# Tile 0 in place of tile 7 gathers its v rows, paced within the groups

## The chip, the cores and the metric

The kernel runs on one core of a Trainium2 chip. Its engines are TensorE (PE in the profile; its weight loads are PEld), VectorE (DVE), ScalarE (ACT), GpSimd (POOL) and SyncE (SP), which starts most transfers; 16 DMA engines move the data. Each engine works through its own queue in order and waits at semaphores. The metric is the device time of one execution in microseconds, the median of several runs.

## The reference

One inference step of a one-layer encoder, for 1024 prompt tokens and 64 sample tokens. Two attention branches are computed, gated and projected back, and then the PEER experts are added. The attention is not touched here. The expert part, cut to what matters:

```python
def peer_tokens(h, w_q, keys, u, v):
    T = h.shape[0]
    q = (h @ w_q).reshape(T, PEER_HEADS, 2, PEER_D_KEY // 2)
    s = jnp.einsum('thcd,hcnd->thcn', q, keys).astype(jnp.float32)
    s1, i1 = lax.top_k(s[:, :, 0], PEER_TOPK)
    s2, i2 = lax.top_k(s[:, :, 1], PEER_TOPK)
    ...
    g = jax.nn.softmax(top, axis=-1).astype(h.dtype)
    act = jax.nn.gelu(jnp.einsum('td,thkd->thk', h, u[idx]), approximate=False)
    return jnp.einsum('thk,thkd->td', g * act, v[idx])

x = x + peer_ffn(rmsnorm(x, norm_ffn), peer_w_q, peer_keys, peer_u, peer_v)
y = rmsnorm(x, norm_final)
```

The lines left out take the 16 best of the sums s1 + s2 and the experts idx that they belong to. There are 16384 experts, each a row of 1024 numbers in u and one in v. Each token has 8 heads with 16 experts, so 128 rows of u and 128 rows of v.

## The kernel before, in words

The 1088 tokens are nine tiles: tiles 0 to 7 are 128 prompt tokens each, tile 8 the 64 sample tokens. The first part of the program works in three groups of three tiles (GROUPS, called group 0, 1 and 2 here): norm, projections, differential attention, latent attention, output projection, then queries and scores against the keys. The second part is two dense passes (PASSES).

For the experts, a tile goes through three jobs, which Python generators emit piece by piece between other instructions.

- **Route** (route_job, line 463, queue "r"): VectorE finds the best 16 experts of each head and writes their numbers and gates to DRAM.
- **Dots** (dots_job, line 338, queue "d"): for each of 128 columns GpSimd gathers one row of u for every token (gather, line 326: 128 rows of 4 KB, 512 KB), and VectorE multiplies it with the token and sums it up (line 357). The rows land in tiles named gb, four buffers, and in groups 1 and 2 also in gm, three more. Behind the last one comes the gelu, and the weights go to DRAM (wgtd). Tile 8 takes 64 columns.
- Then v has to be summed up with these weights. Seven tiles do it densely: **build** (build_job, line 366, queue "b") reads the weights back and makes one-hot matrices on VectorE (oh, lines 401 and 402), weighted ones on ScalarE and VectorE (w, lines 407 and 410), and matmuls (line 417) that spread a token's 128 weights over all 16384 experts; ScalarE copies the result out (lines 421 and 423) and it goes to DRAM as Ad. A build has 16 steps of 24 matmuls. A dense pass then multiplies these matrices with the whole of v: per tile 16 x 48 matmuls (line 1204), which add up in PSUM. For the tile TR, nine sixteenths of the built matrix stay on chip, in Ares.
- Tiles 8 and 7 (VGATHER) do it by **v rows** instead (vgather_job, line 435, queue "d"): 64 and 128 gathers of rows of v, each added to an accumulator by VectorE (line 452).

Group 1 works off the routes and dots of group 0's tiles, group 2 those of group 1's, and the dense passes those of group 2's. spread (line 295) sets how many dots are to come in how many units of other work, pump (line 298) hands the jobs their turns as the units go by, and behind (line 315) ties each dot to the VectorE instruction in front of it, so that it is not moved forward. A scheduler then orders all engines' instructions.

Pass 0 takes tiles 0, 1 and 2, pass 1 tiles 3, 4, 5 and 6. In between, need (line 1159) demands that all tiles of the next pass are routed, dotted and built. Pass 1 takes all eight banks of PSUM for its four sums, and so also those that a build uses. finish (line 427) adds nothing: it norms a row block and writes y. The tile that stands last in VGATHER is normed at the very end (late).

```python
rate["d"] = left["dots"] / max(left["units"], 1.0)      # in pump
left["units"] -= us
...
for ip, tiles in enumerate(PASSES):
    ...
    if ip + 1 < len(PASSES):
        need(PASSES[ip + 1])
```

## Time and profile before

| | us |
|---|---|
| median of 3 runs | 4514.58 (4502.89 to 4516.19) |
| the profiled execution | 4539.65 |
| its span, from the first to the last instruction | 4537.8 |
| TensorE busy in the span | 3806.4 (84%) |
| VectorE busy | 3297.0 (73%) |
| GpSimd busy | 2025.7 (45%) |
| ScalarE busy | 1671.7 (37%) |

The span has six stages. Group 0 ends at 655 us, group 1 at 1786, group 2 with its routing scores at 3002, pass 0 at 3633; pass 1 begins at 3727 and its last matmul ends at 4433. Busy shares over the whole span mix these stages, so they are read by stage.

### The profile page before, as it was taken

What the parts mean: (1) busy time and instruction counts of PE and PEld (TensorE: products, weight loads), DVE (VectorE), ACT (ScalarE), POOL (GpSimd) and SP (SyncE); (2) the same over time, 40 slices, a digit from 0 to 9 for tenths busy, and PEclk for the clock granted to TensorE, in tenths of its full rate; (3) what the DMA queues carried; (4) which work ended last, traced back from release to release, by engine and by line L of the source; (5) the groups of instructions that cost most, each with busy time, mean ns of one, the idle gap of its engine ahead of it and who ended that gap; (6) DMA issues with size and microseconds to landing.
All of it is one profiled execution on the core that took longest, in us unless ns stands there. A gap on an engine that the chain in (4) does not pass through costs nothing.

```text
span 4537.8 us, 56234 instructions
## 1 busy us (share of the span) xinstructions
PE 3806.4 (84%) x19017; PEld 2996.9 (66%) x19017; DVE 3297.0 (73%) x7224; ACT 1671.7 (37%) x3720; POOL 2025.7 (45%) x1353
## 2 busy tenths in 40 slices
PE   6998988888688788887868877889989949999990
PEld 6977887556466565664546666667767737888880
DVE  4043457977678867796776777679997787878776
ACT  3344622035345513322454455145323432322320
POOL 3412331453446542153444656502476446556454
PEclk9967999986788898998768888989999969999995
DMA  5421244996768795697776767978989889989887
GB/s 178 169 88 55 77 167 166 363 341 222 248 231 284 246 345 226 227 345 275 239 252 232 259 231 257 351 257 279 346 297 323 299 294 339 354 318 357 318 322 255
DMA packets 467592, 1183.16 MB, mean 261 GB/s; under 512 B 45352, under 2 KB 218888, under 8 KB 452584
## 3 DMA queue, kind: packets, MB, share of 16 engines
q0 software_dynamic: 184320, 671.17, 41.2%
q1 hardware_dynamic: 282984, 508.41, 32.1%
q8 instruction: 150, 2.46, 0.2%
q14 instruction: 138, 1.13, 0.1%
HBM read 1074.60 MB, written 104.56 MB: 260 GB/s over the span
## 4 chain that ended last, share of the span: by engine, by line
PE 36%; DMA 14%; DVE 14%; issue 8%; ACT 4%; POOL 4%; SPq 0%; another core or an unknown queue 0%; POOLq 0%; DVEq 0%; ACTq 0%
PE acc_ps L1204 14%; PE mm L166 9%; DMA gb<-in_peer_u,beidx 4%; DVE gb L357 4%; POOL gb L332 3%; DMA Ad<-stage 3%; DMA gb<-in_peer_v,beidx 3%; PE mm L826 2%; PE mm L417 2%; DVE gm L357 2%; PE mm L951 2%; PE sc L794 1%; PE sc L792 1%; DMA gm<-in_peer_u,beidx 1%; PE tp L757 1%
## 5 line engine op out<-in xcount | busy, mean ns | idle before, releaser
L332 POOL DMA_INDIRECT gb<-in_peer_u,beidx x758 | 1111.5, 1466 | 1312.0 <-DVE gb L357 732.5
L357 DVE SCALAR_TENSOR_TENSOR gb<-gb,h2r 128x1024 f32<-128x1024 f32 x758 | 917.7, 1219 | 156.1 <-DMA gb<-in_peer_u,beidx 133.7
L332 POOL DMA_INDIRECT gm<-in_peer_u,beidx x330 | 426.4, 1292 | 515.2 <-DVE gm L357 292.3
L1204 PE MATMUL acc_ps<-vhi,alo 128*128 128x512 f32 x1792 | 563.8, 396 | 20.9 <-DVE alo L1198 20.9
L1204 PE MATMUL acc_ps<-vlo,ahi 128*128 128x512 f32 x1792 | 560.8, 396 | 17.8 <-DVE vlo L1185 17.7
L1204 PE MATMUL acc_ps<-vhi,ahi 128*128 128x512 f32 x1792 | 559.3, 395 | 17.7 <-ACT ahi L1197 15.9
L357 DVE SCALAR_TENSOR_TENSOR gm<-gm,h2r 128x1024 f32<-128x1024 f32 x330 | 402.4, 1219 | 33.1 <-DMA gm<-in_peer_u,beidx 27.4
L1204 PEld LDWEIGHTS acc_ps<-vhi,alo 128*128 128x128 f32 x1792 | 340.3, 191 | 95.8 <-DVE alo L1198 25.6
L1204 PEld LDWEIGHTS acc_ps<-vlo,ahi 128*128 128x128 f32 x1792 | 340.2, 191 | 94.7 <-DVE vlo L1185 24.6
L1204 PEld LDWEIGHTS acc_ps<-vhi,ahi 128*128 128x128 f32 x1792 | 341.6, 191 | 90.0 <-ACT ahi L1197 16.5
L332 POOL DMA_INDIRECT gb<-in_peer_v,beidx x192 | 271.1, 1412 | 224.6 <-DVE gacc L452 137.7
L417 PE MATMUL mm<-w,oh 128*128 128x128 bf16 x2688 | 243.4, 244 | 146.6 <-DVE oh L401 75.3
L166 PE MATMUL mm<-h,wraw 128*128 128x384 f32 (+1 forms) x1024 | 318.6, 471 | 16.3 <-ACT qd L738 12.4
L1183 ACT CAST vhi<-vraw 128x1024 fp32r<-128x1024 f32 x256 | 266.3, 1053 | 170.9 <-DMA vraw<-in_peer_v 106.5
L417 PEld LDWEIGHTS <-oh 128*128 128x128 bf16 x2688 | 200.1, 110 | 194.2 <-DVE oh L401 94.1
L452 DVE SCALAR_TENSOR_TENSOR gacc<-gb,vwgt,gacc 128x1024 f32<-128x1024 f32 x192 | 246.4, 1283 | 101.7 <-DMA gb<-in_peer_v,beidx 97.9
L1197 ACT CAST ahi<-araw 128x1024 fp32r<-128x1024 f32 x103 | 108.0, 1049 | 566.9 <-PE acc_ps L1204 504.2
L1185 DVE TENSOR_TENSOR vlo<-vraw,vhi 128x1024 fp32r<-128x1024 f32 x256 | 304.9, 1214 | 3.2 <-ACT vhi L1183 3.2
L178 POOL TENSOR_TENSOR wlo<-wraw,whi 128x2048 fp32r<-128x2048 f32 (+1 forms) x42 | 186.7, 4447 | 262.0 <-ACT whi L177 256.4
L407 ACT ACTIVATE w<-oh,a3f 128x128 bf16<-128x128 bf16 x896 | 280.8, 429 | 44.3 <-DVE oh L402 28.1
L166 PEld LDWEIGHTS mm<-h,wraw 128*128 128x128 f32 x1024 | 197.5, 195 | 126.5 <-ACT qd L738 13.3
L166 PE MATMUL mm<-wraw,h 128*128 128x256 f32 (+1 forms) x960 | 236.6, 403 | 39.9 <-ACT vt L719 28.1
(381 smaller groups left out, 7189.7 us busy)
## 6 DMA issues: line engine op xcount, KB each, us to landing
vraw<-in_peer_v SPq DMA_DIRECT2D x256, 512.0 KB
wraw<-in_w_in SPq DMA_DIRECT2D x66, 1024.0 KB
araw<-Ad SPq DMA_DIRECT2D x103, 512.0 KB
Ad<-stage SPq DMA_DIRECT2D x48, 1024.0 KB
wraw<-in_w_a SPq DMA_DIRECT2D x12, 1024.0 KB
wraw<-in_w_b SPq DMA_DIRECT2D x12, 1024.0 KB
wraw<-in_w_out SPq DMA_DIRECT2D x12, 1024.0 KB
wraw<-in_w_pq SPq DMA_DIRECT2D x12, 1024.0 KB
```

The costliest lines, as they stand in the source:

```text
L166: PE.matmul(out, lhsT=L[0], rhs=R[0], start=start, stop=stop)
L178: G.tensor_tensor(lo[:, :n], raw[:, :n], hi[:, :n].bitcast(F32), op=ALU.subtract)
L332: G.indirect_dma_start(out=gb, out_offset=None, in_=src, in_offset=bass.IndirectOffsetOnAxis(ap=idx, axis=0))
L357: behind(V.scalar_tensor_tensor(gb, gb, 1.0, h2, op0=ALU.mult, op1=ALU.mult, accum_out=act[:, k:k + 1]))
L407: S.activation(w3[:, 0, x // 2, :, x % 2], oh2[:, x // 2, :, x % 2], AF.Copy, scale=a3f[:, tt + x:tt + x + 1])
L417: PE.matmul(pv[:, j, :], lhsT=oh1[:, x // 2, :, x % 2], rhs=w3[:, i, x // 2, :, x % 2], start=i == 0, stop=i == 2)
L452: behind(V.scalar_tensor_tensor(acc, gb, wgt[:, k:k + 1], acc, op0=ALU.mult, op1=ALU.add))
L826: PE.matmul(po[:nq, :128], lhsT=PT[:kw, b, :nq], rhs=Vt[:kw, b, :], start=b == 0, stop=b == nb - 1)
L1183: S.copy(hi, raw)
L1185: V.tensor_tensor(lo, raw, hi.bitcast(F32), op=ALU.subtract)
L1197: S.copy(av, rv)
L1204: PE.matmul(pst[t][:, ds], lhsT=L[:, i, :], rhs=R[:, ds], start=c == 0 and i == 0 and L is ahi and R is vb[i][0], stop=c == 15 and i == 7 ...
```

## The change

Tile 0 takes the place of tile 7 among the tiles that gather v rows, and tile 7 becomes a dense tile. Pass 0 takes tiles 1, 2 and 3, pass 1 tiles 4 to 7, and TR, the last tile to be built, is 7. Tile 0's v rows are queued behind the dots of tile 2, half of them in group 1's count and half in group 2's; the sum, with the residual in it, goes to x1d, and its final norm is emitted with those of pass 0. The pace in the passes is set in two parts: 256 dots in the first 400 units, then 128 dots and v rows in 640. The buffers gm are two and not three, and one gather in three uses them, where it was three in seven.

```diff
--- before.py
+++ after.py
@@ -33,8 +33,8 @@
 MAGIC = float(0x5F3759DF)
 MSC = 96.0 ** -0.5
 GROUPS = ((0, 1, 2), (3, 4, 5), (6, 7, 8))
-PASSES = ((0, 1, 2), (3, 4, 5, 6))
-VGATHER = (8, 7)
+PASSES = ((1, 2, 3), (4, 5, 6, 7))
+VGATHER = (0, 8)
 GN = 384
 SLOT = 3072
 NW = 3
@@ -42,7 +42,7 @@
 PB = 5
 NB = 8
 RC = 9
-TR = 6
+TR = 7
 RATE_R2 = 0.41
 RATE_B, RATE_B2 = 0.3, 0.5
 PUMP_G = (1.1, 1.113, 1.158)
@@ -292,6 +292,8 @@
                 done.add(key)
                 active[q] = None
 
+    plan = []
+
     def spread(units, dots):
         left["units"], left["dots"] = units, left["dots"] + dots
 
@@ -301,6 +303,8 @@
             if traced[i].engine == mybir.EngineType.DVE:
                 anchor["ins"] = traced[i].name
                 break
+        if left["units"] <= 0 and plan:
+            spread(*plan.pop(0))
         rate["d"] = left["dots"] / max(left["units"], 1.0)
         left["units"] -= us
         for q in ("r", "d", "b"):
@@ -325,7 +329,7 @@
 
     def gather(src, idx):
         gturn[0] += 1
-        if cur["more"] and gturn[0] % 7 % 2:
+        if cur["more"] and gturn[0] % 3 == 1:
             gb = cur["more"].tile([128, D], F32, name="gm", tag="gm")
         else:
             gb = cur["gp"].tile([128, D], F32, name="gb", tag="gb")
@@ -425,7 +429,7 @@
             ld(Ad[t, :, n:, t0 // 4:t0 // 4 + 4], stage[:, n:])
 
     def finish(acc, nr, t):
-        if t in VGATHER:
+        if t == 8:
             y = gp.tile([128, D], F32, name="y", tag="gb")
         else:
             y = cur["p2"].tile([128, D], F32, name="y", bufs=1)
@@ -433,12 +437,10 @@
         ld(out_rows("y", t), y[:nr])
 
     def vgather_job(t):
-        while "p2" not in cur:
-            yield
         ns = 128 if t < 8 else 64
-        eidx = bp.tile([128, 128], I32, name="beidx")
-        wgt = bp.tile([128, 128], F32, name="vwgt", tag="bgk")
-        acc = cur["p2"].tile([128, D], F32, name="gacc", bufs=1)
+        eidx = bp.tile([128, 128], I32, name="veidx")
+        wgt = bp.tile([128, 128], F32, name="vwgt")
+        acc = (cur["more"] or cur["p2"]).tile([128, D], F32, name="gacc", tag="gacc", bufs=1)
         if t < 8:
             ld(eidx, eidxd[t])
             ld(acc, x1d[t * 128:t * 128 + 128])
@@ -455,10 +457,10 @@
             oth = cur["gp"].tile([128, D], F32, name="gb", tag="gb")
             ld(oth[0:64], acc[64:128])
             V.tensor_tensor(acc[0:64], acc[0:64], oth[0:64], op=ALU.add)
-        if t == VGATHER[-1]:
+        if t == 8:
             cur["late"] = lambda: finish(acc, tr(t), t)
         else:
-            finish(acc, tr(t), t)
+            ld(x1d[t * 128:t * 128 + 128], acc)
 
     def route_job(t, s_of):
         nr = tr(t)
@@ -562,15 +564,11 @@
         V.reciprocal(gs[:nr], gs[:nr])
         V.tensor_tensor(gk[:nr], gk[:nr], gs[:nr, :, None].to_broadcast([nr, H, 16]), op=ALU.mult)
         ld(gkd[t, :nr], gk[:nr].rearrange("p h k -> p (h k)"))
-        if t not in VGATHER:
-            queues["d"].append((("dots", t), dots_job(t)))
-        elif t not in GROUPS[-1]:
-            queues["d"].append((("dots", t), dots_job(t)))
-        if t == max(x for x in GROUPS[-1] if x < 8):
-            for v in [x for x in VGATHER if x in GROUPS[-1]]:
-                queues["d"].append((("dots", v), dots_job(v)))
-            for v in VGATHER:
-                queues["d"].append((("vg", v), vgather_job(v)))
+        queues["d"].append((("dots", t), dots_job(t)))
+        if t == 2:
+            queues["d"].append((("vg", 0), vgather_job(0)))
+        if t == 8:
+            queues["d"].append((("vg", 8), vgather_job(8)))
 
     for g, tiles in enumerate(GROUPS):
         cur["g"] = g
@@ -581,7 +579,7 @@
         if g:
             nbs = [t + 1 if t < 8 else 5 for t in tiles]
             spread(2.6 * 14 * len(tiles) + 3.9 * 2 * 24 + (H + MH) * sum(PUMP_G[g] * (1 + n * 0.5) for n in nbs),
-                   128 * len(GROUPS[g - 1]))
+                   128 * len(GROUPS[g - 1]) + 64)
         loc = {t: i * 128 for i, t in enumerate(tiles)}
         ptiles = [t for t in tiles if t < 8]
         nblk = ptiles[-1] + 1
@@ -1131,7 +1129,8 @@
         gctx.close()
         if g == 0:
             wctx.close()
-            cur["more"] = ph1.enter_context(tc.tile_pool(name="gm", bufs=3))
+            cur["more"] = ph1.enter_context(tc.tile_pool(name="gm", bufs=2))
+    drain("d", ("vg", 0))
     cur["more"] = None
     ph1.close()
     p2 = ctx.enter_context(tc.tile_pool(name="p2", bufs=2, reuse_waits="tile"))
@@ -1151,7 +1150,8 @@
     cur["rp"], cur["rs"] = rpt, rst
     cur["Ares"] = Ares
     rate["r"], rate["b"] = RATE_R2, RATE_B2
-    spread(16 * 8 * 1.3 * sum(len(x) for x in PASSES), sum((128 if t < 8 else 64) for t in GROUPS[-1] + VGATHER))
+    spread(400, 256)
+    plan.append((640, 128))
     gfin = p2.tile([128, D], F32, name="gfin", bufs=1)
     ld(gfin, bcast_rows(A["norm_final"], D))
     cur["gfin"] = gfin
@@ -1215,10 +1215,11 @@
                     V.tensor_tensor(sacc[:, ds], ps, sacc[:, ds], op=ALU.add)
         for t in tiles[nps:]:
             finish(sacc, 128, t)
-        for t in tiles[:nps]:
+        for t in tiles[:nps] + ((0,) if ip == 0 else ()):
             xr = p2.tile([128, D], F32, name="araw")
             ld(xr, x1d[t * 128:t * 128 + 128])
-            V.tensor_tensor(xr, pst[t], xr, op=ALU.add)
+            if t:
+                V.tensor_tensor(xr, pst[t], xr, op=ALU.add)
             finish(xr, 128, t)
         if ip + 1 < len(PASSES):
             need(PASSES[ip + 1])
```

What a stretch of VectorE's queue holds, before and now, counted in its order (an alo is the lower half of one dense tile's matrix; pass 0 has 48 of them, pass 1 64):

| stretch of VectorE's queue | dots | v rows | builds |
|---|---|---|---|
| group 1, norm to norm | 384, now 384 | 0, now 64 | 2.00, now 1.78 |
| group 2, to its last residual add | 362, now 357 | 0, now 64 | 3.00, now 2.22 |
| to the first alo | 22, now 27 | 0, now 0 | 0.06, now 0.06 |
| pass 0, first to 48th alo | 153, now 154 | 0, now 0 | 1.28, now 1.22 |
| 48th to 49th alo | 42, now 36 | 0, now 0 | 0.66, now 0.72 |
| 49th to 52nd alo | 12, now 92 | 0, now 0 | 0, now 1.00 |
| 52nd to last alo | 113, now 38 | 140, now 64 | 0, now 0 |
| behind the last alo | 0, now 0 | 52, now 0 | 0, now 0 |

VectorE, between pass 0 and pass 1. The last step of tile 6's build among the dots of tile 8 (L357; L361 is their gelu's product), before:

```order
L401 TENSOR_TENSOR oh_27997<-iota_100,ixT 128x1024
L410 TENSOR_TENSOR w_28001<-oh_27998,a_26808 128x1024 x2
L357 SCALAR_TENSOR_TENSOR gb,act<-gb,h2r 128x1024
L194 TENSOR_TENSOR rs_t<-rs_y 128x1
L357 SCALAR_TENSOR_TENSOR gb,act<-gb,h2r 128x1024 x2
L195 TENSOR_TENSOR rs_t<-rs_t,rs_v 128x1
L357 SCALAR_TENSOR_TENSOR gb,act<-gb,h2r 128x1024
L196 SCALAR_TENSOR_TENSOR rs_y<-rs_t,rs_y 128x1
L357 SCALAR_TENSOR_TENSOR gb,act<-gb,h2r 128x1024
L204 SCALAR_TENSOR_TENSOR y<-araw,rs_y,gfin 128x1024
L361 TENSOR_TENSOR act<-act,bgk 128x64
```

VectorE at the same place now: the alo of pass 1's second tile (that of its first stands eleven rows earlier), the dots of tile 7, and the begin of tile 7's build (the dots behind the product at L365 are those of tile 8):

```order
L1198 TENSOR_TENSOR alo<-araw,ahi 128x1024
L361 SCALAR_TENSOR_TENSOR gb,act<-gb,h2r 128x1024 x62
L365 TENSOR_TENSOR act<-act,bgk 128x128
L361 SCALAR_TENSOR_TENSOR gb,act<-gb,h2r 128x1024 x3
L405 TENSOR_TENSOR oh_27945<-iota_100,ixT 128x1024
L406 TENSOR_TENSOR oh_27946<-iota_100,ixT 128x1024
L387 CAST a_27921<-aT 128x128
L361 SCALAR_TENSOR_TENSOR gb,act<-gb,h2r 128x1024
L389 CAST a3f<-a_27921 128x128
L391 TENSOR_TENSOR aT<-aT,a_27921 128x128
```

Before, the last build is over with these rows, and pass 1 follows. Now a row of 62 dots of tile 7 stands there, the gelu's product behind it, and the one-hots (oh) of a whole build begin only after that.

TensorE, at the end of the last build (mm<-w,oh) and the begin of pass 1 (acc_ps), before:

```order
L417 MATMUL mm<-w_28001,oh_27997 128x128
L417 LDWEIGHTS oh_27997
L417 MATMUL mm<-w_28001,oh_27997 128x128
L1204 MATMUL acc_ps<-vhi,ahi 128x512 x2
L1204 MATMUL acc_ps<-vlo,ahi 128x512 x2
L1204 MATMUL acc_ps<-vhi,alo 128x512 x2
```

TensorE now: from the last matmul of tile 6's build (oh_26965) through the transposes (bsrc) into tile 7's:

```order
L421 LDWEIGHTS oh_26965
L421 MATMUL mm<-w_26969,oh_26965 128x128
L379 MATMUL mm<-identR,bsrc 128x128 x3
L421 LDWEIGHTS oh_27945
L421 MATMUL mm<-w_27949,oh_27945 128x128
L421 LDWEIGHTS oh_27945
```

and from the end of tile 7's build into pass 1:

```order
L421 LDWEIGHTS oh_29059
L421 MATMUL mm<-w_29063,oh_29059 128x128
L1204 MATMUL acc_ps<-vhi,ahi 128x512 x2
L1204 MATMUL acc_ps<-vlo,ahi 128x512 x2
L1204 MATMUL acc_ps<-vhi,alo 128x512 x2
```

In both, no matmul of pass 1 stands ahead of the last build's last one. Now two builds end there, tile 6's and, behind its own transposes, the whole of tile 7's.

VectorE at the end of the program, behind the last alo, before (gacc are v rows of tile 7, rs_v to rs_y the small steps of a final norm):

```order
L452 SCALAR_TENSOR_TENSOR gacc<-gb,vwgt,gacc 128x1024 x4
L189 TENSOR_SCALAR rs_v<-rn_ss 128x1
L190 TENSOR_SCALAR rs_t<-rs_v 128x1
L1221 TENSOR_TENSOR araw<-acc_ps,araw 128x1024
L191 TENSOR_SCALAR rs_y<-rs_t 128x1
L192 TENSOR_SCALAR rs_v<-rs_v 128x1
L194 TENSOR_TENSOR rs_t<-rs_y 128x1
L452 SCALAR_TENSOR_TENSOR gacc<-gb,vwgt,gacc 128x1024
L195 TENSOR_TENSOR rs_t<-rs_t,rs_v 128x1
L196 SCALAR_TENSOR_TENSOR rs_y<-rs_t,rs_y 128x1
L452 SCALAR_TENSOR_TENSOR gacc<-gb,vwgt,gacc 128x1024
```

VectorE at the end of the program now:

```order
L195 TENSOR_TENSOR rs_t<-rs_t,rs_v 128x1
L196 SCALAR_TENSOR_TENSOR rs_y<-rs_t,rs_y 128x1
L204 SCALAR_TENSOR_TENSOR y<-araw,rs_y,gfin 128x1024
L1222 TENSOR_TENSOR araw<-acc_ps,araw 128x1024
L189 TENSOR_SCALAR rs_v<-rn_ss 128x1
L190 TENSOR_SCALAR rs_t<-rs_v 128x1
L191 TENSOR_SCALAR rs_y<-rs_t 128x1
L192 TENSOR_SCALAR rs_v<-rs_v 128x1
L194 TENSOR_TENSOR rs_t<-rs_y 128x1
```

The v rows between the steps of the norms are gone; the norms of the last dense tiles follow each other.

## Rows read from the trace of the kernel before

**Rows 1.** Windows by stage: length; busy PE, PEld, DVE, ACT, POOL; clock, DMA share

```profile
655.00:1786.00 1131.00, 935.98 (x4470) 679.20 (x4468) 878.47 (x2312) 405.26 (x1044) 495.71 (x385) 0.87 0.75 269
1786.00:3002.00 1216.00, 987.76 (x5172) 734.92 (x5172) 912.85 (x2139) 486.48 (x1270) 541.45 (x384) 0.84 0.75 263
3002.00:3633.00 631.00, 586.34 (x2832) 472.58 (x2832) 563.38 (x1352) 262.74 (x418) 283.52 (x161) 0.95 0.86 301
3633.00:3727.00 94.00, 29.25 (x243) 23.77 (x241) 75.75 (x143) 40.35 (x121) 44.90 (x35) 0.57 0.86 293
3727.00:4433.00 706.00, 700.57 (x3072) 577.72 (x3072) 554.18 (x622) 193.83 (x188) 398.13 (x274) 0.99 0.91 333
4433.00:4538.00 105.00, 0.00 (x0) 0.00 (x0) 70.94 (x108) 4.60 (x8) 50.29 (x42) 0.51 0.74 255
```

**Rows 2.** VectorE in 4433:4538: group of v rows, timeline of the last

```profile
L452 DVE SCALAR_TENSOR_TENSOR gacc<-gb,vwgt,gacc 128x1024 f32<-128x1024 f32 x45 | 57.7, 1283 | 28.7 <-DMA gb<-in_peer_v,beidx 28.5
...
4527.75 1.28 DVE L452 SCALAR_TENSOR_TENSOR gacc<-gb,vwgt,gacc 128x1024 f32<-128x1024 f32 x1 [0.79 <-DMA gb<-in_peer_v,beidx]
```

**Rows 3.** Chain of waits of 4433:4538: the shortest gather (start us, us, what)

```profile
4522.76 4.90 DMA gb<-in_peer_v,beidx
```

**Rows 4.** Timeline of TensorE around the pass boundary (start us, us, instruction, idle before)

```profile
3572.24 0.23 PE L417 MATMUL mm<-w,oh 128*128 128x128 bf16 x1
...
3633.26 1.55 PE L417 MATMUL mm<-w,oh 128*128 128x128 bf16 x24
...
3708.81 2.29 PE L417 MATMUL mm<-w,oh 128*128 128x128 bf16 x20 [0.23 <-DVE w L410]
3726.88 1.22 PE L1204 MATMUL acc_ps<-vhi,ahi 128*128 128x512 f32 x2 [15.78 <-ACT ahi L1197]
```

**Rows 5.** Timeline of ScalarE at the end: two Squares of final norms

```profile
4449.48 1.06 ACT L202 ACTIVATE y<-araw 128x1024 f32<-128x1024 f32 x1 [30.98 <-DMA out_y_p<-y]
...
4529.12 1.06 ACT L202 ACTIVATE y<-gacc 128x1024 f32<-128x1024 f32 x1 [32.44 <-DVE gacc L452]
```

**Rows 6.** Groups by line of VectorE in 1367:1404: a fast stretch of dots

```profile
L357 DVE SCALAR_TENSOR_TENSOR gb<-gb,h2r 128x1024 f32<-128x1024 f32 x12 | 14.4, 1219 | 0.0
L357 DVE SCALAR_TENSOR_TENSOR gm<-gm,h2r 128x1024 f32<-128x1024 f32 x9 | 11.1, 1232 | 2.0 <-issue 1.9
```

**Rows 7.** Groups by line of VectorE in the gap, 3633:3727: the dots

```profile
L357 DVE SCALAR_TENSOR_TENSOR gb<-gb,h2r 128x1024 f32<-128x1024 f32 x36 | 43.5, 1218 | 11.0 <-DMA gb<-in_peer_u,beidx 11.0
```

**Rows 8.** Timeline: weights of tiles 0, 6 ready; first build matmul of 0

```profile
1089.26 0.28 DVE L361 TENSOR_TENSOR act<-act,bgk 128x128 f32<-128x128 f32 x1
...
1104.65 0.22 PE L417 MATMUL mm<-w,oh 128*128 128x128 bf16 x1 [1.25 <-ACT w L407]
...
3524.26 0.29 DVE L361 TENSOR_TENSOR act<-act,bgk 128x128 f32<-128x128 f32 x1 [0.38 <-ACT act L360]
```

**Rows 9.** Timeline of ScalarE in the gap: weights of three build steps

```profile
3657.87 2.48 ACT L407 ACTIVATE w<-oh,a3f 128x128 bf16<-128x128 bf16 x8
...
3663.88 2.49 ACT L407 ACTIVATE w<-oh,a3f 128x128 bf16<-128x128 bf16 x8
...
3705.77 2.48 ACT L407 ACTIVATE w<-oh,a3f 128x128 bf16<-128x128 bf16 x8 [1.67 <-DVE oh L402]
```

**Rows 10.** Groups by line of VectorE in group 1 (two builds): products, one-hots

```profile
L410 DVE TENSOR_TENSOR w<-oh,a 128x1024 bf16<-128x1024 bf16 x64 | 41.7, 687 | 0.0
...
L401 DVE TENSOR_TENSOR oh<-iota,ixT 128x1024 bf16<-128x1024 bf16 x32 | 22.0, 687 | 16.1 <-PE mm L417 13.6 <-PE tp L1034 1.1 <-ACT ixT L377 0.9
```

**Rows 11.** Chain of waits of group 1, then of group 2, by line

```profile
by line: PE mm L166 18.2%; DMA Ad<-stage 7.6%; issue 5.0%; DVE gb L357 2.9%; PE mm L951 2.8%; PE mm L826 2.7%; PE sc L794 2.7%; PE mm L417 2.6%; PE tp L757 2.5%; DVE gm L357 2.4%; PE sc L792 2.2%; ACT w L407 1.8%; PE sc L800 1.8%; ACT P L81
...
by line: PE mm L166 17.5%; issue 8.8%; DVE gb L357 6.3%; DMA Ad<-stage 5.2%; PE mm L826 4.4%; DVE gm L357 4.4%; DMA gb<-in_peer_u,beidx 4.2%; DMA gm<-in_peer_u,beidx 3.6%; PE mm L417 3.2%; PE mm L951 3.0%; PE sc L794 2.8%; PE sc L792 2.5%; 
```

**Rows 12.** Waits of 1786:3002: GpSimd's pause (us, times, longest)

```profile
POOL gb L332 <- DVE idx L470: 138.4, 1, 138.4
```

**Rows 13.** Timeline of GpSimd in the tail: one gather's descriptors

```profile
4433.19 0.94 POOL L332 DMA_INDIRECT gb<-in_peer_v,beidx  x1 [0.30 <-issue]
```

## The prediction

> **What bounds the kernel now.** I read the busy time by stage first, since the share over the whole span averages six stages with different limits [rows 1]. In group 1 (655 to 1786 us) and group 2 (1786 to 3002) TensorE is busy for 83% and 81%, VectorE for 78% and 75%, the DMA engines for 75%: nothing is full, and the time comes from engines that wait for each other in turn. In dense pass 0 (3002 to 3633) all three stand near 90%. Between the passes, from 3633 to 3727, TensorE has 29 us of work in 94 us. Dense pass 1 (3727 to 4433) is TensorE alone, 700.6 us busy of 706 at the full clock. After it come 105 us without one matmul.
>
> Those last 105 us are the thing to look at first. VectorE works there on rows of peer_v for tile 7: 45 of them are left when the dense pass is over [rows 2], and the last one starts at 4527.75. From that, 95 us for 45 gives 2.1 us a row, although the instruction itself is 1.28 us: the row waits for its gather, which takes from 4.90 us (from GpSimd's start to landing) upwards [rows 3], and only four buffers are in turn.
>
> The second place is the boundary between the passes. The order in front shows that TensorE's queue has all of the last build ahead of the first matmul of pass 1. In the trace the last build's matmuls run from 3572.24 to 3711.1, the last dense matmuls of pass 0 end at 3633.3, and pass 1 begins at 3726.88, 93.5 us later [rows 4]. So what is left to do for the last-built tile when pass 0 ends is paid in full.
>
> **The change part by part: the end.** The rows of tile 7 leave the tail, and none is put in their place: the table of counts has 52 v rows behind the last alo before, and 0 now. What is then left behind the last matmul is one residual add and one norm. The final norm takes from its Square at 4529.12 to the end of the span at 4537.8, 8.7 us [rows 5], and with the add of 1.2 us that is 10. Four tiles share one y buffer, so I take 14. If the writes of y are as slow as now, where a Square waited 30.98 us for one [rows 5], it is 35. From 105 us this gains 91 (70 to 95).
>
> **The gap between the passes.** Tile 7 becomes a dense tile and the last to be built. It needs 128 dots and a build before TensorE may go on. The new pace asks for 256 dots in the first 400 units of pass 0, but in the order that VectorE gets, pass 0 holds 154 dots and before it held 153. With 27 of tile 5 still to come when the pass begins, and 128 of tile 6, only 26 of tile 7 are within pass 0. The order rows show the rest: 36 beside the end of build 6, 4 more, then 62 in one row with nothing between them, then the gelu weights, then all of build 7, and only then pass 1. Step by step, from the last dense matmul of pass 0:
> - the rest of build 6, with 36 dots beside it: 3633.3 to 3711.1 now [rows 4], 78 us again (0.72 of a build with 36 dots, before 0.66 with 42);
> - 66 dots alone. The nearest row is the tail, where four buffers also turn with nothing else to load: 2.1 us, 139 us. Bounds: in group 1, 21 dots went in 37 us with three buffers more [rows 6], 1.76 each, 116 us; in the gap itself 36 took 94 us beside a build [rows 7], 2.6 each, 172 us;
> - from the last dot to the first matmul of the build (gelu, product, a write to DRAM and back, transposes, one-hots): 15.4 us for one tile, from 1089.26 to 1104.65, and 48.0 for another, from 3524.26 to 3572.24 [rows 4, 8], where the queue was full of dense loads. In the gap it is not: 18;
> - build 7, 16 steps. A step without dots takes 6.0 us (ScalarE's weights at 3657.87 and 3663.88); with dots between, the seven from 3657.87 to 3705.77 are 8.0 apart [rows 9]. Ten steps have 26 dots of tile 8 beside them, I take 7.3, and six have none: 73 + 36 = 109 (96 to 139);
> - the start of pass 1: 15.8 us of waiting for a converted tile now [rows 4]; in the new order two converted tiles stand ahead of the 62 dots, so 2 (to 16).
>
> Together 78 + 139 + 18 + 109 + 2 = 346, against 93.5: 252 us longer. The bounds added up are 308 and 453, so 215 to 360 longer. No work covers this: VectorE, GpSimd and the DMA engines do it, and TensorE has nothing else in its queue. The norm of tile 0 that is added here (a load, a Square of about 1 us, a write) lies beside the dots and costs nothing; were it not covered, it would be one such chain, about 9 us.
>
> On the pace of a gather alone, the rows say 4.90 us at best from issue to landing [rows 3]. The Trainium skill ("DMA: Bandwidth & Descriptors", section "Anatomy of one DMA — SWDGE (gpsimd) path") gives a fixed 2.0 us plus the bytes at 436 GB/s, 3.2 us by estimate for the 512 KB of one gather. With four buffers in turn that would be some 1.4 us a dot and 92 us for the 66, and the gap 47 us shorter than by the rows. The trace here does not agree with it, so the sum stays with 2.1; the fast case is a rival below.
>
> **The groups.** Each takes 64 v rows more. A v row is 1.28 us on VectorE [rows 2], 82 us for 64. What goes: one build of seven moves from the groups to the gap, 0.22 of it from group 1 and 0.78 from group 2 by the counts. On VectorE a build is 16 + 16 one-hots and 32 products of 0.69 us [rows 10], 44 us. So VectorE gets 72 us more in group 1 and 48 in group 2, 120 in all: that is the price if VectorE is the bound. The chain of waits says less [rows 11]. In group 1 the dots are 2.9 + 2.4% of 1131 us, 60 us for 384, 0.16 us each, and builds (the write of Ad, their matmuls, their weights: 7.6 + 2.6 + 1.8%) 136 us for two, 68 each. In group 2 dots with their gathers are 18.5% of 1216 us, 225 us for 384, 0.59 each, and builds (5.2 + 3.2%) 102 us for three, 34 each. A v row priced like a dot: 64 x 0.16 - 0.22 x 68 = -5, and 64 x 0.59 - 0.78 x 34 = +11, together +6. If only the builds' relief showed it would be -42. There is room for the new rows too: at the start of group 2 GpSimd stands still for 138.4 us until tile 3 is routed [rows 12], and the counts put most of tile 0's second half there. I take +30, nearer to the chain than to the 120, because part of the rows stands among the norms at the end of group 1, where a row that waits for its gather holds the next norm up. Six buffers in turn in place of seven I leave inside this range.
>
> Pass 0 keeps its counts and so its 631 us, pass 1 keeps its 3072 matmuls and its 706; fewer gathers beside pass 1 can give at most the 5 us that TensorE was idle there.
>
> **Sum.** +252 - 91 + 30 = +191 us. The profiled execution took 4539.65 us (span 4537.8), 25 us above the median of the three runs; added to the median of 4514.58 this gives 4706 us.
>
> **The rivals.**
> - Forecast, 0.62: the gap opens by about 250 us and the tail gives 91 back. Its own range is 4640 to 4780.
> - VectorE decides the groups, 0.16: all 120 us are on the path, +252 - 91 + 120 = +281, 4796 us. For it: a dot is already on the chain in group 2 at 0.59 us. Against it: VectorE is free for 22 to 25% there, and a build is relief for three engines.
> - The gathers run free when nothing else loads, 0.16: GpSimd needs 0.94 us for one plus 0.30 to the next [rows 13], VectorE 1.22 [rows 7], so 1.24 us a dot, 82 us for the 66. With steps of 6.0 us and the short chain the gap is 78 + 82 + 16 + 96 + 2 = 274, +181; with -94 at the end and +6 in the groups, +93, 4608 us. For it: fast stretches in group 1. Against it: the tail with the same four buffers. The skill's formula above would lead to nearly this.
> - Not slower, 0.06: the groups give back more than the gap takes. The write of Ad holds the chain for 7.6% and 5.2%, 149 us in both groups [rows 11]; if the build that leaves, and the later places of the others, took all of that away while the new rows vanish in GpSimd's pause, then with the low gap 215 - 95 - 149 = -29, 4486 us. It decides only if the groups gain over some 120 us even with the gap at its low end. Against it: one build of five leaves them, not all.
>
> A change of this kernel is told from none at about 0.3%, 14 us. Faster by more than that needs nearly all of the last case: 0.04; the same 0.03; slower 0.93. The range goes from a little above the fast-gather case to just above the VectorE case: 4605 to 4810. Beyond it lie half of the fast case's chance at the most and the last case.
>
> **What would show it.** Right: on TensorE some 340 us without dense matmuls between the passes; in it VectorE with 60-odd dots in a row about 2.1 us apart, then 16 build steps; under 35 us behind the last dense matmul; pass 0 within 2% of 631 us. Wrong: a gap under 270 us, or pass 0 much longer because the dots are waited for there, or groups that differ from 1131 and 1216 us by more than 60 each. The forecast falls if TensorE starts pass 1 with build 7 undone.

## The result and the profile after

The changed kernel takes 4752.89 us (median of 4 runs, 4743.78 to 4766.84), the kernel before 4508.74 (4 runs, 4500.82 to 4516.19): ratio 1.0525, interval 1.0491 to 1.0559. It is slower by 5%, as forecast. The predicted time, 4706 us, is 47 us short, and the range of 4605 to 4810 holds the measured one.

The windows view of the changed kernel by the same stages as [rows 1] (stretch, length, busy us and count on PE, PEld, DVE, ACT and POOL, granted clock of TensorE, busy share of the DMA engines, GB/s): group 1, group 2, pass 0, the gap, pass 1, the tail.

```profile
655.00:1825.00 1170.00, 930.47 (x4357) 671.74 (x4356) 945.97 (x2354) 392.69 (x1003) 574.65 (x455) 0.86 0.80 289
1825.00:3075.00 1250.00, 959.94 (x4891) 704.95 (x4891) 957.14 (x2151) 447.05 (x1150) 611.82 (x442) 0.82 0.79 276
3075.00:3697.00 622.00, 579.83 (x2819) 468.70 (x2820) 565.41 (x1355) 258.12 (x396) 283.25 (x162) 0.96 0.88 310
3697.00:4035.00 338.00, 79.55 (x644) 66.96 (x642) 228.61 (x410) 102.96 (x305) 157.54 (x122) 0.51 0.73 245
4035.00:4732.00 697.00, 696.93 (x3075) 576.76 (x3073) 351.59 (x374) 193.51 (x191) 192.47 (x100) 1.00 0.59 206
4732.00:4744.00 12.00, 0.00 (x0) 0.00 (x0) 6.52 (x29) 2.19 (x4) 0.00 (x0) 0.64 0.22 72
```

| stage | before | after | difference | predicted |
|---|---|---|---|---|
| groups 1 and 2 | 2347 | 2420 | +73 | +30 (-42 to +120) |
| pass 0 | 631 | 622 | -9 | 0 |
| gap | 93.5 | 338.5 | +245 | +252 (215 to 360) |
| pass 1 | 706 | 697 | -9 | 0 |
| tail | 105 | 12 | -93 | -91 (-95 to -70) |
| sum | | | +207 | +191 |

The spans of the two profiled executions differ by 4744.3 - 4537.8 = 206.5 us, the medians by 244. The profiled execution of before (4539.65) lies 31 us above the median of before, that of the change (4746.06) 7 us below its own, and that is the other 38. The groups' 2347 us of before are one reading of a quantity that varies: profiles of three kernels below that have the same work in groups 1 and 2 show 2324, 2337 and 2350. Four more profiles with the groups of the change show 2417 to 2434. So the groups grew by something between 70 and 97 us; the means of the two sets, 2340 and 2424, differ by 84.

**The gap, step by step.** The windows view of the changed kernel within the gap: the rest of build 6, the dots alone, the chain to the next build, build 7.

```profile
3697.00:3770.00 73.00, 30.18 (x258) 26.06 (x255) 67.45 (x136) 39.56 (x108) 35.64 (x28) 0.53 0.95 329
3770.00:3917.00 147.00, 0.00 (x0) 0.00 (x0) 91.17 (x158) 4.09 (x6) 85.96 (x67) 0.50 0.81 272
3917.00:3943.00 26.00, 0.87 (x3) 0.61 (x4) 6.54 (x14) 0.98 (x4) 8.32 (x7) 0.50 0.44 132
3943.00:4035.00 92.00, 48.49 (x383) 40.29 (x383) 63.45 (x105) 58.33 (x190) 27.62 (x22) 0.50 0.51 166
```

TensorE's timeline at the corners of these stretches (start us, us, instruction, idle time before and what ended it): the last matmul of build 6, the transposes of tile 7, build 7's first and last ones, and the first of pass 1. It answers to [rows 4].

```profile
3767.20 2.72 PE L421 MATMUL mm<-w,oh 128*128 128x128 bf16 x24 [5.64 <-ACT stage L427]
3938.04 0.87 PE L379 MATMUL mm<-identR,bsrc 128*128 128x128 f32 x3 [168.12 <-DMA bsrc<-wgtd]
3943.05 0.27 PE L421 MATMUL mm<-w,oh 128*128 128x128 bf16 x1 [4.14 <-ACT w L411]
...
4032.81 2.50 PE L421 MATMUL mm<-w,oh 128*128 128x128 bf16 x22 [0.34 <-DVE w L414]
4035.08 0.96 PE L1204 MATMUL acc_ps<-vhi,ahi 128*128 128x512 f32 x2
```

The 168 us in which TensorE stands still are the dots of tile 7 and the write of their weights. Groups by line of VectorE in the second stretch (busy us, mean ns | idle before them):

```profile
L361 DVE SCALAR_TENSOR_TENSOR gb<-gb,h2r 128x1024 f32<-128x1024 f32 x70 | 85.7, 1225 | 45.9 <-DMA gb<-in_peer_u,beidx 45.6
```

70 dots stand there (66 were reckoned), each of 1.22 us, and the time between them is the wait for the gather, as in the tail of before [rows 2]. The last 64 of them start between 3791.1 and 3915.0, 1.97 us apart. Ahead of these lies one hole, shown by VectorE's timeline (only the rows around it) and by the waits of the same stretch (waiting line <- what it waits for: us, times, longest):

```profile
3775.75 1.23 DVE L361 SCALAR_TENSOR_TENSOR gb<-gb,h2r 128x1024 f32<-128x1024 f32 x1 [1.63 <-DMA gb<-in_peer_u,beidx]
...
3786.20 0.15 DVE L189 TENSOR_SCALAR rs_v<-rn_ss 128x1 f32<-128x1 f32 x1 [9.21 <-ACT y L202]
```

```profile
ACT y L202 <- DMA out_y_p<-y: 14.5, 1, 14.5
POOL gb L336 <- DVE rs_y L196: 11.9, 1, 11.9
```

This is the norm of tile 0, the fourth in a row. Its Square may not write y before the third tile's y has left for DRAM, VectorE waits 9.2 us for the Square with the dots queued behind it, and GpSimd stands still for 11.9 us, since all four buffers are full. The run below with tile 0's rows in pass 1 has no norm of tile 0 at this place, and no such hole: 73 dots take 141 us there, 1.93 each, where the change takes 147 for 70.

### The profile page after: what moved, and what is told of

The parts are those of the page before. It is cut to its first block, busy times and chain, and to the rows that moved or that the text cites. A ratio compares the mean times of both kernels' runs of the same rounds, so it can differ in the third digit from the quotient of the medians.

```text
span 4744.3 us, 56273 instructions
## 1 busy us (share of the span) xinstructions
PE 3813.0 (80%) x19017; PEld 2997.0 (63%) x19017; DVE 3297.5 (70%) x7224; ACT 1675.0 (35%) x3720; POOL 2031.4 (43%) x1353
## 5 line engine op out<-in xcount | busy, mean ns | idle before, releaser
L336 POOL DMA_INDIRECT gb<-in_peer_u,beidx x832 | 1180.0, 1418 | 1295.0 <-DVE gb L361 790.7
L361 DVE SCALAR_TENSOR_TENSOR gb<-gb,h2r 128x1024 f32<-128x1024 f32 x832 | 1004.0, 1219 | 187.9 <-DMA gb<-in_peer_u,beidx 143.8
L336 POOL DMA_INDIRECT gm<-in_peer_u,beidx x256 | 341.9, 1336 | 334.0 <-DVE gm L361 130.2
L336 POOL DMA_INDIRECT gb<-in_peer_v,veidx x149 | 242.5, 1627 | 406.5 <-DVE gacc L454 295.0
L361 DVE SCALAR_TENSOR_TENSOR gm<-gm,h2r 128x1024 f32<-128x1024 f32 x256 | 312.1, 1219 | 41.3 <-DMA gm<-in_peer_u,beidx 33.3
L1198 DVE TENSOR_TENSOR alo<-araw,ahi 128x1024 fp32r<-128x1024 f32 x103 | 125.8, 1222 | 277.0 <-ACT ahi L1197 276.1
```

What stands on the lines that cost most here:

```text
L336: G.indirect_dma_start(out=gb, out_offset=None, in_=src, in_offset=bass.IndirectOffsetOnAxis(ap=idx, axis=0))
L361: behind(V.scalar_tensor_tensor(gb, gb, 1.0, h2, op0=ALU.mult, op1=ALU.mult, accum_out=act[:, k:k + 1]))
L1198: V.tensor_tensor(alo.rearrange("p i (q t) -> p i q t", t=4), rv, av.bitcast(F32), op=ALU.subtract)
```

## The experiments

Times of other kernels are compared by their ratio to the kernel before on the same chip; the change stands at 1.0525. Differences of ratios are turned into us with 4509. The diffs show the lines that matter; lines from different places stand one below the other, and `...` marks lines left out. Where the price of a part is read from the stages, it comes from one profile each, and the groups of one program vary by some 20 us between profiles.

**The buffer in the groups.** The kernel before with the change's gather buffers:

```diff
-        if cur["more"] and gturn[0] % 7 % 2:
+        if cur["more"] and gturn[0] % 3 == 1:
-            cur["more"] = ph1.enter_context(tc.tile_pool(name="gm", bufs=3))
+            cur["more"] = ph1.enter_context(tc.tile_pool(name="gm", bufs=2))
```

> The kernel before with the gather buffers of the changed one: two gm instead of three, one gather in three into them. It tells what of the 73 us that groups 1 and 2 got longer (1131 + 1216 = 2347 before, 1170 + 1250 = 2420 after) is the buffer and what the 128 v rows. My theory: the rows are the price, six buffers in place of seven cost the 768 dots of the groups little: groups 2347 to 2362 us, total within 15 us of before (4509). Rival: the buffer is most of it: groups 2395 or more, total about 4555.

Ratio 1.0002 (0.9976 to 1.0027); groups 1113 + 1211 = 2324 us. The third buffer is worth nothing that these runs can show to the dots of the groups; the rival falls.

**The rows out, pace and all.** The changed kernel without the v rows of tile 0 and without their share in the pace:

```diff
-        for k in range(ns):
+        for k in range(ns if t else 0):
             gb = gather(A["peer_v"], eidx[:, k:k + 1])
-                   128 * len(GROUPS[g - 1]) + 64)
+                   128 * len(GROUPS[g - 1]))
```

> The changed kernel without the 128 v rows of tile 0 in the groups (its experts' sum is left out of tile 0's output; its norm stays). Theory: the groups fall back below before, since a build less is in them: 73 us of growth plus some 42 us of relief, so 115 us or 0.9 us a row; groups about 2305, total about 4638. Rival one, VectorE is the bound: 128 x 1.28 = 164 us less, groups 2256, total 4589. Rival two, the rows are nearly free and the two buffers are the price: under 30 us less, total over 4720. The gap stays at 338 in all.

Ratio 1.0141 (1.0101 to 1.0181), 173 us under the change; groups 1058 + 1197 = 2255, so 166 us less, the number of rival one. But two things went out together: the pace asks for fewer turns, so that the dots come later too, and one build and not 1.78 stands in group 1. The next two take this apart.

**The additions out, the gathers in.**

```diff
+            m = 1 if t == 0 else D
-            behind(V.scalar_tensor_tensor(acc, gb, wgt[:, k:k + 1], acc, op0=ALU.mult, op1=ALU.add))
+            behind(V.scalar_tensor_tensor(acc[:, :m], gb[:, :m], wgt[:, k:k + 1], acc[:, :m], op0=ALU.mult, op1=ALU.add))
```

> The changed kernel with tile 0's 128 v rows gathered as before, but VectorE adds only the first of the 1024 columns of each (the rest of tile 0's experts' sum is left out). The rows cost 166 us in groups 1 and 2 (2421 with them, 2255 without). Theory A, VectorE's time is the price (128 x 1.28 = 164 us): the groups fall to about 2265, total about 4600. Theory B, the waits and the transfers of the gathers are the price, not the additions: the groups stay over 2370, total over 4700. In between (about 2320) both have a share.

Ratio 1.0341 (1.0308 to 1.0375), 83 us under the change; groups 1166 + 1199 = 2365. Neither theory: VectorE's additions are worth 56 us of the groups, nearly all of it in group 2 (1250 to 1199), and 5 in group 1 (1171 to 1166).

**The rows out, the pace kept.** Each row takes its turn and does nothing, so that all else is emitted where the change has it:

```diff
         for k in range(ns):
+            if t == 0:
+                left["dots"] -= 1
+                yield
+                continue
             gb = gather(A["peer_v"], eidx[:, k:k + 1])
```

> The changed kernel without tile 0's v rows (their sum is left out of tile 0's output), but each row still takes its turn in the pace, so that all dots and builds are emitted at the same places as in the change (1.78 builds in group 1, where the run without rows and without their turns had 1.00). Groups 1 and 2 took 2421 us with rows, 2365 with rows of one column, 2255 without rows and turns. Theory, the faster pace and the builds that it moves among the norms at the end of group 1 are the other 110 us: groups 2340 to 2365, total about 4660. Rival, the gathers of the rows and their transfers are those 110 us: groups about 2255, total about 4590.

Ratio 1.0262 (1.0236 to 1.0288), 119 us under the change; groups 1126 + 1176 = 2302. Between the two again. The three runs together give, from the stages: 119 us for the rows (56 for the additions, 63 for the gathers), and 2302 - 2255 = 47 us for the pace and the builds that it moves. From the ratios the same parts are 119 (83 and 36) and 55. So the rows and the moved builds are separable, and the split of the rows is rough.

Where each acts can be seen. In group 1 it is the output projection, where TensorE takes matmuls of build 2 and of the projection in turn and stands still with ScalarE's copies of built pieces, which wait until an earlier piece has been written to Ad. From the first add of x to the last norm the change takes 84 us (1660 to 1744), the run with one-column additions 72 (1669 to 1741), this run 53 (1656 to 1709), and the kernel before, which has no build at this place, 46 (1672 to 1718). ScalarE's waits for these writes in that stretch, of the change, of the run with one-column additions, and of this run:

```profile
ACT stage L427 <- DMA Ad<-stage: 33.1, 3, 17.0
```

```profile
ACT stage L427 <- DMA Ad<-stage: 21.3, 3, 13.6
```

```profile
ACT stage L427 <- DMA Ad<-stage: 9.3, 3, 4.4
```

So 31 of the 45 us by which group 1 is longer with the rows stand here, beside a wait for the writes that is 24 us longer; with the gathers alone it is 12 us longer. The same wait summed over the whole of group 1 does not tell this, as the lines of the change, of this run, and of the kernel before show:

```profile
ACT stage L427 <- DMA Ad<-stage: 71.0, 11, 17.0
```

```profile
ACT stage L427 <- DMA Ad<-stage: 36.2, 10, 7.0
```

```profile
ACT stage L423 <- DMA Ad<-stage: 70.6, 10, 15.9
```

The kernel before has no rows in its groups and waits as long as the change, at other places. At the start of group 2 it is VectorE. The windows view from the norm to the first scores of the change, of the run with one-column additions, and of this run (busy PE, PEld, DVE, ACT, POOL):

```profile
1825.00:2157.00 332.00, 237.83 (x1028) 172.72 (x1029) 280.11 (x957) 57.29 (x148) 145.48 (x117) 0.86 0.85 298
```

```profile
1820.00:2091.00 271.00, 238.75 (x1033) 174.20 (x1033) 189.64 (x911) 55.43 (x147) 94.38 (x93) 0.92 0.87 320
```

```profile
1780.00:2043.00 263.00, 231.83 (x1024) 168.63 (x1025) 206.12 (x898) 57.53 (x148) 73.94 (x59) 0.93 0.73 260
```

The stretch is 61 us longer with the full additions, and 8 with the gathers alone. The kernel before takes 322 us for it (1786 to 2108), with 276 more matmuls in it, 0.7 of a build's 384: it had more of a build at this place, and no rows. TensorE's longest wait in it, first in the change, then in the run without rows:

```profile
PE sc L792 <- DVE Qd L146: 50.4, 1, 50.4
```

```profile
PE sc L794 <- ACT Qd L853: 16.7, 1, 16.7
```

VectorE splits the queries for the scores behind routing and 64 additions of 1.28 us, and TensorE waits for that. The run with one-column additions has no such wait.

**The dots of tile 7.** Half of them left out:

```diff
+        if t == 7:
+            V.memset(act[:, :64], 0.0)
-        for k in range(ns):
+        for k in range(64 if t == 7 else 0, ns):
             gb = gather(A["peer_u"], eidx[:, k:k + 1])
-    spread(400, 256)
+    spread(400, 192)
```

> The changed kernel with 64 of tile 7's 128 dots (the other 64 weights are set to zero, so tile 7's output lacks half its experts). Theory: dots of tile 7 that do not fit into pass 0 are paid one by one in the gap, at the 2.05 us of the trace after (135 us for 66): 64 x 2.05 = 131 us less, gap 207, pass 0 unchanged at 622, total about 4622. Rival: something else holds the gap (the chain to the build, the transfer engines), so that the fewer dots are only partly felt: gap over 260, total over 4675.

Ratio 1.0219 (1.0182 to 1.0257), 138 us under the change, at 4625.33 us (4622 was expected). The gap:

```profile
3712.00:3924.00 212.00, 80.41 (x655) 67.53 (x654) 154.36 (x287) 102.75 (x306) 77.50 (x61) 0.53 0.72 243
```

338 - 212 = 126 us for 64 dots, 1.97 us each: they are paid one by one.

**Eight gather buffers in the passes.**

```diff
-RC = 9
+RC = 5
+        elif "p2" in cur and gturn[0] % 2:
+            gb = cur["p2"].tile([128, D], F32, name="gx", tag="gx", bufs=4)
```

> The changed kernel with four more gather buffers in the passes (half the gathers go there; they take four of the nine sixteenths of tile 7's matrix that stayed on chip). In VectorE's queue pass 0 then has 195 dots and 1.84 builds in place of 154 and 1.22, and some 22 dots of tile 7 stand alone instead of 66. Theory, four buffers in turn set the 2.05 us of a dot: a dot alone takes 1.3 to 1.6 us, the gap is about 10 + 62 + 35 + 26 + 92 = 225 us, pass 0 up to 30 us longer because its transfers grow: total about 4670. Rival, the transfer engines set the pace (they are 80 to 90% busy in the gap's dots): a dot stays at 2 us, and pass 0 grows by what the gap loses: total within 30 us of 4753.

4669.47 us, ratio 1.0323 (1.0281 to 1.0365), 91 us under the change. Pass 0 and the gap:

```profile
3078.00:3734.00 656.00, 597.51 (x3005) 479.24 (x3006) 626.85 (x1459) 279.69 (x472) 339.72 (x206) 0.96 0.92 335
3734.00:3957.00 223.00, 54.06 (x460) 45.84 (x458) 161.68 (x306) 77.86 (x231) 109.02 (x82) 0.52 0.75 269
```

The total is as expected, the working only in part. Pass 0 holds 199 dots in place of 159 and is 34 us longer, the gap 115 shorter. But in the gap's first stretch, where the other loads still run, a dot took 1.75 us (58 in 101 us) and not 1.3 to 1.6, with this share of the transfer engines (0.98):

```profile
3733.00:3834.00 101.00, 7.66 (x77) 6.50 (x75) 92.18 (x187) 19.62 (x37) 69.47 (x51) 0.53 0.98 373
```

So with four buffers it was their number that set the pace, and with eight the transfers are next.

**The place of the rows.** Tile 0's v rows in pass 1 in place of the groups:

```diff
-        if t == 2:
+        if t == 8:
             queues["d"].append((("vg", 0), vgather_job(0)))
-                   128 * len(GROUPS[g - 1]) + 64)
+                   128 * len(GROUPS[g - 1]))
-    plan.append((640, 128))
+    plan.append((640, 256))
-            ld(x1d[t * 128:t * 128 + 128], acc)
+            finish(acc, tr(t), t)
...
```

> The changed kernel with tile 0's v rows behind the dots of tile 8 in dense pass 1, where VectorE is busy for 352 of 697 us, in place of the groups. It undoes one part, the place of the rows. Theory: the groups are those of the run without rows (2255), pass 1 takes 232 gathers in some 700 us and hides them, gap 320 to 350, tail 12 to 20: total about 4600, 150 us under the change. Rival: the rows in pass 1 make its transfers late as in the kernel before (0.91 busy) and leave a tail of 50 us or more, total over 4650.

4589.98 us, ratio 1.0163 (1.0127 to 1.0199). Groups 2261, and the gap, pass 1 and the tail:

```profile
3528.00:3878.00 350.00, 74.16 (x627) 61.57 (x627) 251.11 (x433) 97.39 (x293) 178.26 (x143) 0.53 0.80 268
3878.00:4576.00 698.00, 698.00 (x3076) 577.86 (x3073) 486.81 (x468) 195.10 (x195) 340.18 (x204) 1.00 0.79 285
4576.00:4588.00 12.00, 0.03 (x1) 0.00 (x0) 6.56 (x29) 2.19 (x4) 0.00 (x0) 0.70 0.21 66
```

Pass 1 takes all 192 rows and stays at 698 us: it had room for them, at no price. The gap holds 143 dots in place of 122 and is 12 us longer. The place of the rows, with their turns in the pace of the groups, is worth 163 us.

**More dense work ahead of the boundary.** Passes of four and three tiles:

```diff
-PASSES = ((1, 2, 3), (4, 5, 6, 7))
+PASSES = ((1, 2, 3, 4), (5, 6, 7))
-RC = 9
+RC = 8
```

> The changed kernel with passes of four and three tiles (1 to 4, then 5 to 7) in place of three and four; the fourth tile of pass 0 is summed up by VectorE, since PSUM has no room for it, and one sixteenth of tile 7's matrix leaves the chip for that sum. It gives TensorE a tile's work (174 us) ahead of the boundary and puts nothing else in: in VectorE's queue 307 dots and 2.94 builds then stand in pass 0, none of a build behind it. Theory, the gap is long only because nothing covers tile 7's dots and build: VectorE has 307 x 1.31 for the dots, 129 for builds, 234 for vlo and alo and some 100 more, 865 us, so pass 0 takes about 900, the gap 20, pass 1 525, and the groups stay at 2421: total about 4530. Rival, a dot in a pass costs what it costs now (159 in 622 us, 3.9 each): pass 0 about 1200, total over 4750, and the work only moves.

4780.54 us, ratio 1.0602 (1.0564 to 1.064). The total is the rival's, though pass 0 is 1114 us and not 1200, and what holds it is not the price of a dot. Pass 0, what is left of the gap, pass 1, and TensorE's longest wait in pass 0:

```profile
3070.00:4184.00 1114.00, 817.55 (x4181) 661.89 (x4182) 845.10 (x1800) 356.36 (x700) 458.78 (x312) 0.86 0.76 261
4184.00:4236.00 52.00, 11.25 (x50) 9.04 (x49) 26.94 (x78) 14.58 (x19) 1.70 (x1) 0.64 0.44 161
4236.00:4760.00 524.00, 523.96 (x2304) 433.43 (x2303) 298.66 (x293) 175.70 (x172) 168.47 (x71) 1.00 0.65 231
```

```profile
PE mm L379 <- DMA bsrc<-wgtd: 189.8, 2, 103.6
```

The gap is 52 us, but the two passes and the gap together take 1690 in place of 1657. TensorE's queue now has the transposes of the last two builds in the middle of pass 0, and twice it waits there for the dots, 190 us in all, with dense matmuls queued behind. The work came under other work in the order and not in time.

**Better versions.** The kernel before with the eight buffers, the same edit:

```diff
-RC = 9
+RC = 5
+        elif "p2" in cur and gturn[0] % 2:
+            gb = cur["p2"].tile([128, D], F32, name="gx", tag="gx", bufs=4)
```

> The kernel before with eight gather buffers in the passes in place of four (they take four of the nine sixteenths of tile 6's matrix that stayed on chip). In VectorE's queue pass 0 then has 183 dots and 1.69 builds (153 and 1.28), the gap 0.25 of a build (0.66), the tail 40 v rows (52). Theory, four buffers set the pace of a gather wherever nothing else is full: tail 40 x 1.4 + 10 = 66 us in place of 105, gap 35 in place of 93, pass 0 25 us longer: total about 4445. Rival, the transfer engines set it: tail still about 2 us a row, pass 0 and pass 1 longer by what the rest gains: total 4490 or more.

4447.89 us, ratio 0.9869 (0.9811 to 0.9927): it beats both kernels. Pass 0, the gap, pass 1, the tail:

```profile
2992.00:3636.00 644.00, 597.25 (x2976) 478.78 (x2977) 609.11 (x1427) 279.66 (x488) 318.13 (x192) 0.95 0.90 327
3636.00:3691.00 55.00, 10.55 (x97) 8.92 (x96) 37.30 (x84) 18.91 (x50) 19.35 (x16) 0.56 0.81 287
3691.00:4391.00 700.00, 699.38 (x3072) 578.30 (x3072) 566.30 (x624) 191.86 (x189) 413.60 (x284) 1.00 0.93 345
4391.00:4447.00 56.00, 0.00 (x0) 0.00 (x0) 47.45 (x89) 4.48 (x8) 23.58 (x20) 0.52 0.72 274
```

The gap falls from 93.5 to 55, the tail from 105 to 56, pass 0 pays 13. The gap was taken too low (35), the tail too high (66).

The same with a faster pace in the passes:

```diff
...
-    spread(16 * 8 * 1.3 * sum(len(x) for x in PASSES), sum((128 if t < 8 else 64) for t in GROUPS[-1] + VGATHER))
+    spread(0.8 * 16 * 8 * 1.3 * sum(len(x) for x in PASSES), sum((128 if t < 8 else 64) for t in GROUPS[-1] + VGATHER))
```

> The kernel before with eight gather buffers in the passes (4448 us) and the pace of the passes spread over 0.8 of the units. In VectorE's queue pass 0 has 192 dots and 1.84 builds (183 and 1.69), the gap 0.09 of a build (0.25), the tail 20 v rows (40). Theory, what is left for the boundary and the tail is what costs: gap 55 to about 45, tail 57 to about 40, pass 0 up to 10 us longer: total about 4430. Rival, the transfer engines are full in pass 0 and pass 1, so that earlier gathers only delay the dense loads: within 10 us of 4448.

Ratio 0.9836 (0.981 to 0.9862), whose interval overlaps with that of the one before. Pass 0 grew to 671 us, the gap fell to 49 and the tail to 38: what was taken out of the end went into pass 0, nearly one for one. By the stages the rival is nearer; the two times do not decide it.

Part of the change alone, with eight buffers: tile 0 gathers in the groups, tile 7 gathers too, behind tile 8 as before, six tiles are dense, and the pace in the passes is one again, 512 dots and rows:

```diff
-PASSES = ((1, 2, 3), (4, 5, 6, 7))
-VGATHER = (0, 8)
+PASSES = ((1, 2, 3), (4, 5, 6))
+VGATHER = (0, 8, 7)
-TR = 7
+TR = 6
...
```

> One part of the change alone, with eight buffers in the passes: tile 0 gathers its v rows in the groups as in the change, but tile 7 gathers too, as before, so that only six tiles are dense (passes of three and three) and nothing of tile 7 has to be done before pass 1. Theory: groups 2421 as in the change, pass 0 650, gap 20 to 30 (0.09 of a build), pass 1 523, a tail of some 100 rows x 1.4 + 10 = 150: total about 4430. Rival: pass 1 is then bound by its gathers and their transfers, not by TensorE (over 560 us, or a tail over 220), total over 4500, and gathering a second tile is worth nothing.

4486.64 us, ratio 0.9937 (0.9914 to 0.996): the groups 2422, pass 0 663, gap 63, pass 1 538, tail 139. By the ratio that is 51 us over the 4430 expected, 33 or more of it in the gap, which was taken at 20 to 30; the other stages are within 15 us. It beats the kernel before; its ratio is higher than that of the kernel with eight buffers, with intervals that just overlap.

In this gap almost nothing of a build is left. What TensorE waits for in it, and what ScalarE waits for:

```profile
PE acc_ps L1211 <- ACT ahi L1204: 61.4, 1, 61.4
ACT y L202 <- DMA out_y_p<-y: 52.7, 3, 20.4
```

TensorE waits for the first converted tile (ahi) of pass 1. In ScalarE's queue that conversion stands behind the Squares of pass 0's norms, and these wait, one after the other, until the single y buffer has been written out. The kernel with eight buffers and the faster pace has the same picture in its gap of 49 us (47.4 and 40.1 us). That a second y buffer would shorten these gaps is not shown: it was not tried.

The tail of this run shows gathers with eight buffers and nothing else to load. The windows view, and VectorE's groups by line:

```profile
4342.00:4471.00 129.00, 0.00 (x0) 0.00 (x0) 126.35 (x128) 2.30 (x4) 94.32 (x88) 0.52 0.99 384
```

```profile
L456 DVE SCALAR_TENSOR_TENSOR gacc<-gb,vwgt,gacc 128x1024 f32<-128x1024 f32 x48 | 61.7, 1285 | 1.3
L456 DVE SCALAR_TENSOR_TENSOR gacc<-gx,vwgt,gacc 128x1024 f32<-128x1024 f32 x47 | 60.4, 1284 | 1.3
```

95 rows start between 4341.5 and 4471.0, 1.38 us apart, where the tail of before had 2.1 with four buffers [rows 2]: VectorE is busy for 126 of 129 us, and the transfer engines are full.

The savings put together: passes of four and three, tile 0's rows in pass 1 (that edit is not shown again), seven buffers in the passes:

```diff
-PASSES = ((1, 2, 3), (4, 5, 6, 7))
+PASSES = ((1, 2, 3, 4), (5, 6, 7))
-RC = 9
+RC = 5
+        elif "p2" in cur and gturn[0] % 7 % 2:
+            gb = cur["p2"].tile([128, D], F32, name="gx", tag="gx", bufs=3)
...
-    spread(400, 256)
-    plan.append((640, 128))
+    spread(665, 310)
+    plan.append((400, 202))
```

> A version from the findings: passes of four and three tiles, tile 0's v rows in pass 1 in place of the groups, seven gather buffers in the passes in place of four, and a pace of 310 dots for pass 0. Theory, the three savings add up: groups 2255, pass 0 about 880, gap 20, pass 1 525 with 172 rows beside it, a tail of 20 rows, 38: total about 4370, under both kernels. Rival, pass 0 is bound by its transfers and its dots (1100 us or more): total over 4590.

4521.06 us, ratio 1.0005 (0.9986 to 1.0025): level with the kernel before, 150 us over what was expected. Groups 2255, pass 1 526 and tail 36 came as reckoned or nearly; the gap took 47 and not 20, and pass 0 999 and not 880:

```profile
2910.00:3909.00 999.00, 828.15 (x4179) 667.46 (x4180) 834.67 (x1797) 356.67 (x700) 505.41 (x315) 0.89 0.82 292
```

TensorE's waits in it are spread over the builds' one-hots, weights, copies and transposes and over vlo, none of these above 38 us in sum. What would fill them was not tried.

## Why the prediction was right, and where it was off

**The gap** was right in size and, but for one small term, in its steps: rest of build 6 73 (78 forecast), dots 147 (139), chain 26 (18), build 7 92 (109), start of pass 1 0 (2). The pace of a dot with four buffers, taken from the tail as 2.1 us, was 1.97 outside the one hole; that the dots are paid one by one was shown by leaving 64 of them out (126 us). The build was priced too high: its 16 steps took 92 us, 5.8 each, the price of a step without dots, although 22 gathers ran beside it.

The step on the norm of tile 0 failed: "lies beside the dots and costs nothing". It held the dots up by some 12 us, through the single y buffer and VectorE's queue: at the 1.93 us of the run without this norm the 70 dots would have taken 135 us and not 147. The price named for the uncovered case, 9 us, is near the 9.2 us of VectorE's wait.

**The fast gathers**, the rival at 0.16, did not come about: with four buffers a dot took 1.97 us and not 1.24. With eight buffers and nothing beside it a row took 1.38 us, at 384 GB/s. The formula of the Trainium skill ("DMA: Bandwidth & Descriptors", section "Anatomy of one DMA — SWDGE (gpsimd) path"), by which four buffers would give an estimated 1.4 us a dot, does not agree with the 1.97; its 436 GB/s is of the size of the 384 that eight buffers reach.

**The tail** was right: 12 us for the 14 forecast, and pass 1 gave back 9 us where 5 at most were allowed.

**The groups** were the term that was mis-sized: +70 to +97 where +30 was taken, within its bounds. The step that failed is "a v row priced like a dot", 0.16 us in group 1 and 0.59 in group 2 from the chain of waits. The runs show 45 us for 64 rows in group 1 (0.70 each) and 74 in group 2 (1.16 each), 119 where the chain gave 48. A chain's share is what the work there cost along one path; it does not say what the next 64 of them will cost. The relief from the build that left was larger too: the groups with one build less and no rows take 2255 us in place of 2347, 92 less (69 against the reading of 2324), where 42 was forecast. The third part was not in the sum at all: the higher pace for the rows moves dots and builds forward, build 2 among the projection and the norms of group 1, some 47 us. So -92 + 47 + 119 = +74 (73 by the table; each part is a difference of single profiles).

**The rival that VectorE decides the groups**, at 0.16, put all 120 us of VectorE's added time on the path. The measured growth lies between its +120 and the forecast's +30. As a mechanism it held in part: the additions of the rows are 164 us on VectorE and cost 56, nearly all of them at the start of group 2, where TensorE waits for VectorE; the rest came from the gathers and the moved builds. That the groups would give back more than the gap takes, the rival at 0.06, did not happen.

"There is room for the new rows too", at GpSimd's pause of 138 us, was the wrong engine's room: VectorE was the one that TensorE waited for behind that pause. And the reason given for the +30, that a row which waits for its gather holds the next norm up, was not what happened: between 1560 and 1825 VectorE waited 5 us in all ahead of the 64 rows. The norms were late since the output projection was, beside ScalarE's longer waits for the writes of Ad.

**In part it was luck** that the sum came so near. By stages it is +207 against the +191 forecast: the groups were taken 43 us too low, the two passes 18 too high, the gap 7 too high, and within the gap the norm's 12 us were hidden by build 7's 17. By the medians it is +244, and 4752.89 us lies about midway between the forecast's 4706 and the VectorE rival's 4796.

## What to carry to other kernels

Before taking work out of a tail, look for what its replacement must precede: here 128 dots and a build stood ahead of a pass in TensorE's queue, and what did not fit before was paid in full. Where gathers stand alone, reckon their pace by the buffers that turn, and try more buffers before moving the work: the kernel before with eight of them beats both. When a boundary is cleared of its large work, see what is left there: here a chain of norms through one buffer. Work of an off-path engine goes where the wait of the bounding engine does not pass through it (pass 1 took 128 rows at no price, the groups at 119 us), and room on the engine that issues it says nothing about room on the one that consumes it.
